# First stage of a transformer layer: modulation by row sums on three engines, two pairs of heads projected side by side

## The chip, the cores and the metric

One core of one Trainium2 chip. The metric is the device time of one execution in microseconds (us), the median over several. The engines are named as the profile names them: PE is TensorE (matmul), PEld its weight loads, DVE is VectorE, ACT is ScalarE, POOL is GpSimd, SP is SyncE, which here issues all DMAs (SPq is its queue). An engine works through its instructions in the order in which the program holds them, and waits at the first one that isn't ready.

## What is computed

One layer with stick-breaking attention and a SwiGLU FFN, float32, 2048 tokens of width 1024, 16 heads of 64, FFN width 2816. What the change touches is the first line and the modulation `h`:

```python
mod_all = jnp.einsum('bd,lde->lbe', jax.nn.silu(c), ada_w) + ada_b[:, None]
sh_m, sc_m, gt_m, sh_f, sc_f, gt_f = jnp.split(mod_all[i][:, None, :], 6, axis=-1)
h = rms_norm(x, norm_g[i, 0]) * (1 + sc_m) + sh_m
qkv = (h @ w_qkv).reshape(b, s, 3, N_HEADS, HEAD_DIM)      # then stick-breaking attention, by 128 queries
...
x = x + gt_m * rms_norm(y, norm_g[i, 1])                   # y: attention output @ w_o
h = rms_norm(x, norm_g[i, 2]) * (1 + sc_f) + sh_f
x = x + gt_f * rms_norm(swiglu_ffn(h, ...), norm_g[i, 3])
```

`sh_m` and `sc_m` are needed before the first projection: c (1024) times 2048 columns of `ada_w`, 8 MB, each element of which is used once. The other four segments come late in the attention.

## The kernel before

Tokens stand in 4 blocks of 512 (`b`), features in 8 tiles of 128 (`k` or `m`), heads in 8 pairs (`p`). Products have float32 precision by a split: each operand is a high part, written by a cast on ACT, and a low part, the rest, written by a subtraction on DVE or POOL; `mm3` (L176 to L178) makes three matmuls of it. A pair's projection `t` is 1 for k, 0 for q, 2 for v; a step (p, b) of `project` is 3 x 8 such triples, each a slice. `STEPS` orders the steps: (0, 0), (1, 0), (0, 1), (0, 2), (0, 3), (1, 1) and so on; the second one, `PARKED`, is of the second pair, and its k, q and v go to DRAM until they are needed. From (0, 1) on slices of projection are dealt out among attention units by a rate (`AHEAD`, `SLICES`, `RATE`); the first score of the attention (`score`, L604) comes after 18 slices of (0, 1). That is the same in both kernels.

The program fixes the order on PE, ACT, DVE and POOL by hand; a DMA is issued by SP in about the program's order, waiting until its tile's buffer is free. Buffers rotate under a tag (`BUFS`): "qkn" has 2, "qt" 3, "ht" 5, "kt" and "v" 7. PSUM has 8 banks: 3 of `accps` ("acc"), 3 of `zps` ("z"), 2 of `tps` ("t").

The first stage, step (0, 0):

- The modulation comes in four pieces of 256 columns (`AQ`), each of shift and scale, 2 MB in two transfers. The chunk for one k-tile is 128 rows (elements of c) by 2 x 256 columns. DVE adds the chunks up, each times its element of silu(c) (`ada_sum`, L724 and L727, 128x512), PE adds what is left along the partitions by matmuls with one column (`ada_direct` L737 with c itself, `ada_rest` L744 with ones), and `ada_cols_done` (L752 to L755) turns that into shift and gain for two feature tiles.
- Block 0 of x is squared on ACT (L167), scaled on DVE (L341), transposed on PE (`x_turn`, L372); `full_high` applies gain and shift on ACT (L782) and casts the high part (L786), `low` subtracts (L791). `weights_high` and `weights_low` (L761, L766) split the pair's three weight tiles.
- PE multiplies tile by tile of features into the three acc banks (`first_products`). SP's order: c, the first piece (2 MB), x (4 x 512 KB), the first weights (512 KB), the small constants, the other weights, the other pieces.

Step (1, 0) follows: its k goes to a z bank. Beside its slices the weights of its v are split, block 1 is squared, spread and shared (`x_square`, `x_spread`, `x_share`: a row of 512 scales, copied to all partitions by a transpose, L363 and L365), block 2 squared, and block 1's tiles are made by `first_norm` (`scale_cols` L383 on DVE and L387 on POOL, `modulate` L400 to L408). Blocks 1 and 3 come with features already along the partitions (`xc`). The evictions of k, q and v are `split` (L507 cast on ACT, L508 on DVE) and L546; `values_turn` (L552 to L557) transposes v. The k and q of (0, 0) are sent into `kt` and `qt` by four DMAs each (L524, L538), and then SP stores block 0's tiles (L482).

Of the kernel before, what the change touches and what calls it, by code (L numbers as in the profile page):

```python
# [39 lines left out]
SLICES = [0, 3 * KC] + [3 * KC + VGAP] * (NPAIR * NB - 2)  # L40


AHEAD = 6 * KC + 6
# [4 lines left out]

AQ = 256
# [25 lines left out]
SQUARE_AT = [(0, 2), (0, 7), (2, 1), (2, 7)]  # L75

NORM_AT = {
    None: [], 1: [(0, 4), (0, 6), (2, 3), (2, 5)],
    2: [(2, 2), (2, 4), (2, 6)], 3: [(2, 2), (2, 4), (2, 6)],
}  # L80
# [27 lines left out]
def hybrid_trunk_kernel(  # L108
# [5 lines left out]
    ada_first: bass.AP,  # L114
# [28 lines left out]
    shift = const.tile([P, 2, KC], F32, name="shift")  # L143
    c_act = const.tile([P, KC], F32, name="c_act")
# [61 lines left out]

    def split_early(p, t, tags):

        raw = raws.pop((p, t))
        if len(tags) == 1:  # L210
            hl = att.tile([P, 2, KC, P], F32R, name=f"w{p}_{t}", tag=tags[0], bufs=BUFS[tags[0]])
            hi, lo = hl[:, 0], hl[:, 1]
        else:
            hi, lo = [
                att.tile([P, KC, P], F32R, name=f"w{p}_{t}_{j}", tag=tag, bufs=BUFS[tag])
                for j, tag in enumerate(tags)
            ]
        nc.scalar.copy(hi, raw)
        nc.vector.tensor_tensor(lo, raw, f32(hi), op=ALU.subtract)
        weights[p, t] = hi, lo  # L220

# [167 lines left out]
    def modulate(hl, b, k):  # L389

        gain, add = g_eff[:, 0, k : k + 1], shift[:, 0, k : k + 1]
# [61 lines left out]
    def project(at):  # L453

        p, b = STEPS[at]
        begun = (p, b) == (0, 0)
# [7 lines left out]
        def product(t):  # L464
            if begun:
                return first_acc[t]
            w = weights[p, t]
            if parked and t == 1:
                acc = zps.tile([P, BT], F32, name=f"pj{p}_{b}_{t}", tag="z")
            else:  # L470
                acc = accps.tile([P, BT], F32, name=f"pj{p}_{b}_{t}", tag="acc")
            ahead = b == NB - 1 and p + 1 < NPAIR
            for k in range(KC):
                if t == 1:
                    if p == 0:
                        first_norm(b, k + (4 if b == 1 else 3))
                    if k == 0 and nb == 3:
                        cols_load(3)
                    if k == 5 and waiting:
                        waiting.pop()()  # L480
                if parked and t == 1 and k % 2 == 0:
                    nc.sync.dma_start(*stores[k // 2])  # L482
                if parked and (t, k) == (1, 6):
                    split_early(1, 2, ["whl"])
                if nb in (1, 3) and t == 1 and k < 4:
                    x_square(nb, k)
                if nb and t == 1 and 2 <= k < 6:
                    x_spread(nb, k - 2)
# [6 lines left out]
                if (t, k) in NORM_AT[nb]:  # L495
                    first_norm(nb, NORM_AT[nb].index((t, k)))
# [200 lines left out]
    chunks, piece_sums, cols_ps = {}, {}, {}  # L697

    ON_PE = {0: (0, KC - 1), 1: (KC - 1,), 2: (KC - 1,), 3: (KC - 1,)}

    def ada_chunk(q, kh):
        ks = range(KC // 2 * kh, KC // 2 * (kh + 1))
        if q == 2:
            for k in ks:
                w = att.tile([P, 2, AQ], F32, name=f"ac{q}_{k}", tag="a", bufs=BUFS["a"])
                nc.sync.dma_start(w, ada_first[q, kh][:, :, k % 4])
                chunks[q, k] = w
            return
        tag = "ht" if (q, kh) == (1, 1) else "qt"
        w = att.tile([P, 2, KC // 2, AQ], F32, name=f"ac{q}_{kh}", tag=tag, bufs=BUFS[tag])  # L710
        nc.sync.dma_start(w, ada_first[q, kh])
        for k in ks:
            chunks[q, k] = w[:, :, k % 4]
# [100 lines left out]
    for k in ada_sums(0):  # L814
        ada_sum(0, k)
# [869 lines left out]
```

## Time and profile before

| | |
|---|---|
| median of 3 runs | 2849.86 us (2848.97 to 2851.37) |
| the profiled execution's own time | 2848.15 us |
| its span on the core | 2845.8 us |
| mean granted PE clock | 0.998 |
| DMA | 521 MB, mean 183 GB/s; 262 to 414 GB/s in the stretches of 10 us of the first 60 |

How to read the rows that are shown below. A row of the timeline has start in us, length in us, engine, line, operation, output and inputs, shape, count, and in brackets the idle time before it and what ended that. A matmul's length overlaps its neighbours'; its cost is the distance to the next start. A row of the waits: who waited for whom, us in total, times, longest. A row of the groups: line, engine, operation, count, busy us and mean ns of one, then idle time before. A row of the stretches: the stretch, its length, then busy us of PE, PEld, DVE, ACT, POOL with counts, granted clock, DMA share, GB/s. A row of the DMA issues: transfer, count, KB each, us from issue to landing (median).

### The profile page before, as it was taken

The page shows a single profiled execution, that of the slowest core. Times are in us where ns is not written, and L with a number is a line of the kernel's source. Part 1 is how long each engine was busy: PE and PEld are TensorE (multiplying, and loading weights), DVE is VectorE, ACT ScalarE, POOL GpSimd, SP SyncE. Part 2 cuts the span into 40 slices and gives each one's busy share as a digit, 9 for nine tenths or more (in the row PEclk, how much of TensorE's full clock was granted, in tenths as well). Part 3 has the DMA queues.
Part 4 walks back from the last instruction along what each step waited for, and adds up shares of the span by engine and source line. Part 5 has one row for each costly group of instructions (what it writes and reads, how often), then busy time and mean ns, then how long its engine had stood idle before and what let it go on. Part 6 is the DMA issues. An engine that isn't in the chain of part 4 may idle for free.

```text
span 2845.8 us, 41691 instructions
## 1 busy us (share of the span) xinstructions
PE 2795.2 (98%) x13792; PEld 2330.7 (82%) x13792; DVE 2028.9 (71%) x2821; ACT 1634.1 (57%) x3273; POOL 1289.3 (45%) x2036
## 2 busy tenths in 40 slices
PE   8899999999999999999999999999999999999998
PEld 6688888888888888887888788888788888888887
DVE  6788888888888888888866766555775665133477
ACT  5787777787787877878645533333433333322343
POOL 2575666676576655666410122222222222544455
PEclk9999999999999999999999999999999999999999
DMA  9874556656665635546289544334353334545565
GB/s 368 283 225 164 185 161 221 211 178 226 193 211 186 216 114 178 193 134 230 95 296 317 195 141 151 119 106 158 124 177 108 111 108 163 191 142 155 179 224 185
DMA packets 240519, 521.03 MB, mean 183 GB/s; under 512 B 22448, under 2 KB 110512, under 8 KB 222640
## 3 DMA queue, kind: packets, MB, share of 16 engines
q1 hardware_dynamic: 240304, 518.38, 56.2%
q8 instruction: 109, 1.79, 0.3%
q14 instruction: 106, 0.87, 0.1%
HBM read 351.04 MB, written 118.49 MB: 165 GB/s over the span
## 4 chain that ended last, share of the span: by engine, by line
PE 86%; DVE 5%; ACT 3%; issue 2%; POOL 2%; DMA 2%; SPq 0%; DVEq 0%; POOLq 0%; ACTq 0%
PE s L176 9%; PE s L178 9%; PE s L177 9%; PE z L604 8%; PE o L683 8%; PE t L655 8%; PE pj L176 5%; PE pj L177 5%; PE pj L178 5%; PE o L177 4%; PE o L176 4%; PE o L178 4%; PE y L178 2%; PE y L176 2%; PE y L177 2%
## 5 line engine op out<-in xcount | busy, mean ns | idle before, releaser
L645 POOL TENSOR_TENSOR a<-a,w 128x512 f32<-128x512 f32 (+3 forms) x640 | 621.1, 970 | 225.2 <-DVE w L638 128.9
L638 DVE TENSOR_TENSOR_SCAN w<-z,c,begin 128x512 f32<-128x512 f32 x384 | 489.3, 1278 | 84.6 <-ACT z L623 62.2
L176 PE MATMUL s<-r,l 128*128 128x512 f32 x1232 | 482.2, 391 | 4.8 <-DVE p L1447 3.9
L178 PE MATMUL s<-r,l 128*128 128x512 f32 x1232 | 479.9, 390 | 0.0
L177 PE MATMUL s<-r,l 128*128 128x512 f32 x1232 | 479.9, 390 | 0.0
L621 ACT ACTIVATE a<-z 128x512 f32<-128x512 f32 (+3 forms) x640 | 347.4, 543 | 170.4 <-PE z L604 137.7
L683 PE MATMUL o<-aT,v 128*128 128x512 f32 (+3 forms) x1280 | 384.3, 381 | 0.1
L671 DVE TENSOR_TENSOR aT<-t,aT 128x512 fp32r<-128x512 f32 (+3 forms) x640 | 358.6, 594 | 23.7 <-ACT aT L665 23.0
L604 PE MATMUL z<-kt,qt 128*128 128x512 f32 (+3 forms) x1280 | 363.0, 365 | 0.1
L665 ACT CAST aT<-t 128x512 fp32r<-128x512 f32 (+3 forms) x640 | 314.1, 534 | 73.4 <-PE t L655 63.2
L623 ACT ACTIVATE z<-z 128x512 f32<-128x512 f32 (+3 forms) x640 | 345.0, 539 | 0.0
L1455 POOL TENSOR_TENSOR one<-p,p 128x512 f32<-128x512 f32 x44 | 71.6, 1627 | 578.1 <-issue 321.7
L176 PE MATMUL pj<-ht,w 128*128 128x512 f32 x768 | 309.1, 402 | 5.0 <-issue 1.4
L655 PE MATMUL t<-begin,a 128*128 128x128 f32 x2176 | 295.2, 273 | 14.3 <-DVE aT L671 13.0
L655 PEld LDWEIGHTS t<-begin,a 128*128 128x128 f32 x2176 | 254.7, 140 | 65.1 <-DVE aT L671 15.5
L177 PE MATMUL pj<-ht,w 128*128 128x512 f32 x768 | 303.4, 395 | 1.8 <-DVE ht L408 0.5
L178 PE MATMUL pj<-ht,w 128*128 128x512 f32 x768 | 302.8, 394 | 0.0
L176 PEld LDWEIGHTS s<-r,l 128*128 128x128 f32 x1232 | 231.7, 188 | 54.8 <-ACT l L1308 2.9
L178 PEld LDWEIGHTS s<-r,l 128*128 128x128 f32 x1232 | 231.6, 188 | 48.4
L177 PEld LDWEIGHTS s<-r,l 128*128 128x128 f32 x1232 | 231.8, 188 | 48.2 <-issue 0.5
L633 DVE TENSOR_TENSOR_SCAN w<-z,begin 128x128 f32<-128x128 f32 (+3 forms) x256 | 208.6, 817 | 76.9 <-ACT z L623 66.0
L604 PEld LDWEIGHTS z<-kt,qt 128*128 128x128 f32 x1280 | 230.3, 188 | 37.8 <-DVE w L633 0.5
(178 smaller groups left out, 4866.6 us busy)
## 6 DMA issues: line engine op xcount, KB each, us to landing
ht<-h_s SPq DMA_DIRECT2D x108, 1024.0 KB, 8.4
wi<-in_win SPq DMA_DIRECT2D x86, 512.0 KB, 4.0
qt<-qn SPq DMA_DIRECT2D x124, 256.0 KB, 4.6
ol_qt<-act_s SPq DMA_DIRECT2D x56, 512.0 KB, 3.7
act_s<-S SPq DMA_DIRECT2D x66, 256.0 KB, 3.9
br<-in_wout SPq DMA_DIRECT2D x66, 256.0 KB, 3.5
h_s<-ht SPq DMA_DIRECT2D x16, 1024.0 KB, 8.3
o_s<-os SPq DMA_DIRECT2D x128, 128.0 KB, 2.8
```

Source lines behind the costliest of these rows:

```text
L176: nc.tensor.matmul(acc, lhs[0], rhs[0], start=first, stop=False, **kw)
L177: nc.tensor.matmul(acc, lhs[0], rhs[1], start=False, stop=False, **kw)
L178: nc.tensor.matmul(acc, lhs[1], rhs[0], start=False, stop=last, **kw)
L604: nc.tensor.matmul(z[:, :n], q[:, e, part, r * P : (r + 1) * P], k[:, e, :n], start=part == 0, stop=part == 1,)
L621: nc.scalar.activation(a[:, :n], z[:, :n], AF.Sigmoid, scale=QK_SCALE)
L623: nc.scalar.activation(z[:, :n], z[:, :n], AF.Sigmoid, scale=-QK_SCALE)
L638: nc.vector.tensor_tensor_scan(rest[:, rev], left[:, rev], begin[:, :BT][:, rev], initial=carries[r], op0=ALU.mult, op1=ALU.bypass,)
L645: nc.gpsimd.tensor_tensor(a[:, :n], a[:, :n], rest[:, 1 : n + 1], op=ALU.mult)
L655: nc.tensor.transpose(pt[:, rb * P : (rb + 1) * P], weighed[i, rb][:, j * P : (j + 1) * P], ident)
L665: nc.scalar.copy(hl[:, 0, t0:], pt[:, t0:])
L671: nc.vector.tensor_tensor(hl[:, 1, t0:], pt[:, t0:], f32(hl[:, 0, t0:]), op=ALU.subtract)
L683: nc.tensor.matmul(acc[:, t0:], lhs, hl[:, part, t0:], start=sc == qb and j == 0 and part == 0, stop=sc == 0 and j == 3 and part == 1,)
```

## The change

- The modulation of the first stage is laid out by features: a row tile `ar` holds 128 features on the partitions, and shift and scale rows of 1024 (1 MB, eight of them). c comes as a row sent to all 128 partitions (`c_rows`, 512 KB). The sum along a row is one DVE instruction with an accumulator output (`row_sum`); for the shift part of tiles 1, 3, 5 and 7 POOL multiplies (`row_product`) and ACT sums (`row_total`). `row_done` makes one tile's shift and gain. PE has no part in it.
- Pairs 0 and 1 are projected side by side: for each feature tile three products for pair 0 (acc banks), then three for pair 1 (z banks). Pair 1's weights are loaded early, two of their low parts are made by POOL.
- Block 1 is loaded, squared and shared within this stage, and its first four tiles are made behind the last products' issue, ahead of the evictions of both pairs. Block 2 is squared in step (0, 1), at its q, not in (1, 0). The late parts of (1, 0) are gone: k's z bank, stores among its slices. SP sends block 0's stores partly within the stage.
- The scores' slices are the same: the 24 that are dealt to (1, 0) become 0, and `AHEAD` falls by 24.

```diff
-SLICES = [0, 3 * KC] + [3 * KC + VGAP] * (NPAIR * NB - 2)
-AHEAD = 6 * KC + 6
+SLICES = [0, 0] + [3 * KC + VGAP] * (NPAIR * NB - 2)
+AHEAD = 3 * KC + 6
...
     def project(at):
-        begun = (p, b) == (0, 0)
+        begun = at < 2
...
-            if parked and t == 1:
-                acc = zps.tile([P, BT], F32, name=f"pj{p}_{b}_{t}", tag="z")
-            else:
-                acc = accps.tile([P, BT], F32, name=f"pj{p}_{b}_{t}", tag="acc")
+            acc = accps.tile([P, BT], F32, name=f"pj{p}_{b}_{t}", tag="acc")
...
-                    if k == 5 and waiting:
-                        waiting.pop()()
+                    if k in (3, 5) and waiting:
+                        waiting.pop(0)()
...
-                if nb in (1, 3) and t == 1 and k < 4:
-                    x_square(nb, k)
-                if nb == 1 and (t, k) in SQUARE_AT:
-                    x_square(2, SQUARE_AT.index((t, k)))
+                square_at = {2: 0, 3: 1}.get(nb)
+                if t == square_at and k < 4:
+                    x_square(nb, k)
...
+    ROW_TAGS = ["whl", "qt", "qt", "qt", "ht", "qt", "qt", "qt"]
+    def row_load(m):
+        rows[m] = att.tile([P, 2, D], F32, name=f"ar{m}", tag=tag, bufs=BUFS[tag])
+        nc.sync.dma_start(rows[m], ada_rows[m])
+    def row_sum(m, seg):
+        w = rows[m][:, seg]
...
+        nc.vector.scalar_tensor_tensor(
+            w, w, 1.0, c_rows, op0=ALU.mult, op1=ALU.mult, accum_out=sums[m][:, seg : seg + 1]
+        )
+    def row_product(m):
+        w = rows[m][:, 0]
+        nc.gpsimd.tensor_tensor(w, w, c_rows, op=ALU.mult)
+    def row_total(m):
+        w = rows[m][:, 0]
+        nc.scalar.activation(w, w, AF.Identity, accum_out=sums[m][:, 0:1])
+    def row_done(m):
+        nc.vector.tensor_tensor(mod[:, :, m], sums.pop(m), b_cols[:, 0:2, m], op=ALU.add)
+        nc.vector.scalar_tensor_tensor(
+            g_eff[:, 0, m : m + 1], mod[:, 1, m : m + 1], 1.0, gc[:, 0, m : m + 1],
+            op0=ALU.add, op1=ALU.mult,
+        )
...
     nc.sync.dma_start(c_act, c)
+    c_rows = att.tile([P, D], F32, name="c_rows", tag="qkn", bufs=BUFS["qkn"])
+    nc.sync.dma_start(c_rows, c_row[0:1].to_broadcast((P, D)))
     nc.scalar.activation(c_act, c_act, AF.Silu)
-    nc.scalar.activation(spare, mhalf, AF.Sigmoid)
-    ada_chunk(0, 0)
-    ada_chunk(0, 1)
+    nc.scalar.activation(c_rows, c_rows, AF.Silu)
     x_load(0)
+    row_load(0)
     load_weights(0, 1)
     nc.sync.dma_start(b_cols, ada_b_cols)
     nc.sync.dma_start(gc, g_cols)
+    row_load(1)
     load_weights(0, 0)
     load_weights(0, 2, "qkn")
...
+    for t in (1, 0, 2):
+        load_weights(1, t, "v")
+    for m in range(2, 5):
+        row_load(m)
...
+    row_sum(0, 1)
+    row_sum(0, 0)
+    row_done(0)
+    weights_high(0, 1)
+    weights_low(0, 1, nc.vector)
+    full_high(0)
+    weights_high(0, 0)
+    low(0)
+    weights_low(0, 0, nc.vector)
+    row_sum(1, 1)
+    row_product(1)
+    weights_high(0, 2)
+    weights_low(0, 2, nc.vector)
+    row_total(1)
+    row_done(1)
+    first_products(0, 0)
+    full_high(1)
+    weights_high(1, 1)
+    weights_low(1, 1, nc.gpsimd)
+    low(1)
+    weights_high(1, 0)
+    weights_low(1, 0, nc.gpsimd)
+    turned_x[2] = x_turn(0, 2)
+    first_products(0, 1)
+    turned_x[3] = x_turn(0, 3)
+    weights_high(1, 2)
+    row_sum(2, 1)
+    weights_low(1, 2, nc.vector)
+    row_sum(2, 0)
+    row_done(2)
+    row_load(5)
+    x_load(1)
+    first_products(1, 0)
+    first_products(1, 1)
+    for m in range(2, KC):
+        full_high(m)
+        if m + 1 < KC:
+            row_sum(m + 1, 1)
+            if m % 2 == 0:
+                row_product(m + 1)
+                row_total(m + 1)
+        low(m)
+        if m + 1 < KC:
+            if m % 2 == 1:
+                row_sum(m + 1, 0)
+            row_done(m + 1)
...
+        first_products(0, m)
+        if m + 2 < KC:
             turned_x[m + 2] = x_turn(0, m + 2)
...
+        if m == KC - 1:
+            x_share(1)
+        first_products(1, m)
+    nc.sync.dma_start(*stores[0])
+    nc.sync.dma_start(*stores[1])
+    for k in range(4):
+        first_norm(1, k)
+    x_load(2)
+    nc.sync.dma_start(*stores[2])
+    nc.sync.dma_start(*stores[3])
     late = late_modulation((2, 3, 4), "wraw", 2, 0, 3, accps, "acc")
```

The evictions of both pairs follow from `project` for the first two steps, which has no slices left in them.

More of the change, by code (lines that the diff above doesn't have):

```diff
@@ L389, in modulate @@
     def modulate(hl, b, k):
-        gain, add = g_eff[:, 0, k : k + 1], shift[:, 0, k : k + 1]
+        gain, add = g_eff[:, 0, k : k + 1], mod[:, 0, k : k + 1]
         if b not in BY_FEATURES:
@@ L783, in full_high @@
             full, turned_x.pop(m), AF.Identity,
-            bias=shift[:, 0, m : m + 1], scale=g_eff[:, 0, m : m + 1],
+            bias=mod[:, 0, m : m + 1], scale=g_eff[:, 0, m : m + 1],
         )
```

202 lines of the change are left out of this document (48 added, 154 removed).

## The prediction

> **What bounds the kernel now.** I read the page, then the waits of PE (TensorE), then the first 130 us engine by engine in order of time, since the change ends there: from the first score on, both kernels issue the same work.
>
> ```profile
> span 2845.8 us, 41691 instructions
> PE 2795.2 (98%) x13792; PEld 2330.7 (82%) x13792; DVE 2028.9 (71%) x2821; ACT 1634.1 (57%) x3273; POOL 1289.3 (45%) x2036
> ```
> ```profile
> PE acol L737 <- DMA ac<-in_ada_first: 6.8, 2, 6.2
> PE t L655 <- DVE aT L671: 5.9, 4, 2.3
> ```
>
> PE is the bound: of 2845.8 us it is idle 50.6. What the first stage can give is the time before PE's first product, its slow products, and little else. The first score is the mark to which I reckon:
>
> ```profile
> 20.56 0.80 PE L176 MATMUL pj<-ht,w 128*128 128x512 f32 x1 [0.67 <-ACT ht L786]
> ...
> 27.24 0.39 PE L177 MATMUL pj<-ht,w 128*128 128x512 f32 x1
> 27.47 0.40 PE L178 MATMUL pj<-ht,w 128*128 128x512 f32 x1
> ...
> 28.70 1.05 PE L744 MATMUL acol<-ones,asum 128*128 128x1 f32 x8 [0.40 <-DVE asum L727]
> ...
> 30.04 0.63 PE L177 MATMUL pj<-ht,w 128*128 128x512 f32 x1
> 30.47 0.63 PE L178 MATMUL pj<-ht,w 128*128 128x512 f32 x1
> ```
> ```profile
> 62.05 0.39 PE L176 MATMUL pj<-ht,w 128*128 128x512 f32 x1
> ...
> 62.73 0.39 PE L176 MATMUL pj<-ht,w 128*128 128x512 f32 x1
> ...
> 72.69 0.60 PE L552 MATMUL vt<-begin,vT 128*128 128x128 f32 x4
> 73.04 0.47 PE L176 MATMUL pj<-ht,w 128*128 128x512 f32 x1
> ...
> 83.15 0.34 PE L604 MATMUL z<-kt,qt 128*128 128x128 f32 x2
> ```
>
> Three products cost 0.68 (62.05 to 62.73), four transposes 0.35 (72.69 to 73.04). In slow stretches a product takes 0.43 (30.04 to 30.47) instead of 0.23. Five tiles of the step (0,1) lie ahead of 72.69, so that step began, and both pairs of heads were done, at 72.69 - 5 x 0.68 = 69.3; the first score came 13.9 later, at 83.15.
>
> **The start.** Its transfers arrive in the order of issue:
>
> ```profile
> 10.00:20.00 10.00, 5.12 (x19) 3.66 (x18) 6.13 (x15) 7.47 (x12) 3.38 (x4) 1.00 1.03 414
> ```
> ```profile
> 9.89 1.06 ACT L167 ACTIVATE xn<-x 128x1024 f32<-128x1024 f32 x1 [5.68 <-DMA x<-in_x]
> ...
> 13.73 1.06 ACT L167 ACTIVATE xn<-x 128x1024 f32<-128x1024 f32 x1
> ...
> 15.07 1.04 ACT L761 CAST w<-wr 128x1024 fp32r<-128x1024 f32 x1 [0.19 <-DMA wr<-in_wqkv]
> ...
> 21.36 0.77 ACT L782 ACTIVATE hf<-xT,shift,g_eff 128x512 f32<-128x512 f32 x1
> 22.17 0.62 ACT L786 CAST ht<-hf 128x512 fp32r<-128x512 f32 x1
> ```
> ```profile
> 21.49 1.23 DVE L766 TENSOR_TENSOR w<-wr,w 128x1024 fp32r<-128x1024 f32 x1
> 22.82 0.69 DVE L791 TENSOR_TENSOR ht<-hf,ht 128x512 fp32r<-128x512 f32 x1
> ...
> 23.95 4.69 DVE L727 SCALAR_TENSOR_TENSOR asum<-ac,c_act,asum 128x512 f32<-128x512 f32 x6
> ```
>
> The rings are full (share 1.03, 414 GB/s). The first x tile (9.88) had 2.5 MB up to its end, the first weights (15.0) 4.5: 2.57 us a MB, so a tile lands at 3.5 + 2.57 x MB. The change puts 0.5 MB of c (one row sent to 128 partitions) where 2 MB of modulation stood: x lands from 6.1 to 9.9, row tile 0 at 12.5, the first weights at 13.8, row tile 1 at 16.3, tile 2 at 25, tile 3 at 27.5. Four squares at 1.28 (9.89 to 13.73) end at 11.3; scaling x ends at 12.9. No row shows a row sum: L727, 0.78 for 512, and 0.54 for 512 more (1.23 less 0.69) make 1.3; not under 1.23, which a product of that size takes without a sum, and not over 2.4, a rival below. Two sums, the closing pair (0.35), L782 and L786 (1.43) give the first product at 12.9 + 2.6 + 0.4 + 1.5 = 17.4, 3.2 sooner.
>
> **Between first product and the end of both pairs** the change sets POOL (GpSimd) beside DVE. That isn't free here:
>
> ```profile
> 68.39 1.44 POOL L387 TENSOR_TENSOR xc<-xc,x 128x512 f32<-128x512 f32 x1
> ```
> ```profile
> 69.17 1.20 DVE L408 TENSOR_TENSOR ht<-xc,ht 128x512 fp32r<-128x512 f32 x1 [0.50 <-ACT ht L406]
> ...
> 75.01 0.68 DVE L408 TENSOR_TENSOR ht<-xc,ht 128x512 fp32r<-128x512 f32 x1
> ```
> ```profile
> L645 POOL TENSOR_TENSOR a<-a,w 128x512 f32<-128x512 f32 x448 | 497.1, 1110 | 172.7 <-DVE w L638 128.9 <-DVE w L633 30.6 <-issue 1.9
> ...
> L204 POOL TENSOR_TENSOR w<-wr,w 128x1024 fp32r<-128x1024 f32 x21 | 50.4, 2400 | 0.0
> ```
>
> The DVE subtraction begun at 69.17 inside POOL's operation ended 0.54 after that one ended (69.83): 512 elements in 0.54, so it had stood still till then; alone it takes 0.68. Two operations that each read two tiles of SBUF run one after the other. POOL's at 1024 cost 2.2 (twice 1.11) to 2.4; I take 2.3. In order: DVE splits the first weights to 17.1; POOL's product of row tile 1 holds the port to 19.4; tile 0's low part 19.95, second weights 21.15, row sum 22.45, third weights 23.6, closing and ACT 25.4, low part 26.1, row sum of tile 2 27.4; POOL's split of pair 1's first weights 29.7; DVE's split of the third 30.85; POOL's second 33.15; row sum 34.4; POOL's product of tile 3 36.7; closing and ACT 38.5; low part of tile 2 39.2. PE, slow till about 30, has its first four parts done by 36.9 and waits till 39. Then it is the bound: two tiles cost it 4 x 2.04 + 0.7 = 8.9, and DVE and POOL together 3 x 1.3 + 1.4 + 0.7 + 2.3 = 8.3. ACT's sum over POOL's product (1.3, a square's pace) closes tile 3 at about 41, when PE needs it at 43; ACT has room there for block 1's squares and the sigmoid table, which move to it. Twelve parts are left, 24.5, four transposed tiles and the share of block 1, 1.75: end E = 39.0 + 26.2 = 65.3, against 69.3. That gain of 4.0 is all there is. The column products that go (such as the eight at 28.70), and the second slow stretch that came behind them, are inside it.
>
> **What comes behind E.** Ahead of the evictions of pair 0's three banks the new order puts the first four tiles of block 1, and these wait for the shared row, whose transposes lie only one part (2.05) before E. The banks of (0,1) are these same ones (before, a z bank kept the steps apart). On ACT (ScalarE), SP and the DMA rings:
>
> ```profile
> 50.41 0.59 ACT L507 CAST kn<-pj 128x512 fp32r<-128x512 f32 x1 [0.35 <-PE pj L178]
> ...
> 57.84 0.58 ACT L507 CAST kn<-pj 128x512 fp32r<-128x512 f32 x1
> ...
> 67.06 0.71 ACT L400 ACTIVATE ht<-xc,shift 128x512 fp32r<-128x512 f32 x1
> 67.68 0.81 ACT L405 ACTIVATE xc<-xc,shift,g_eff 128x512 f32<-128x512 f32 x1
> 68.52 0.62 ACT L406 CAST ht<-xc 128x512 fp32r<-128x512 f32 x1
> ```
> ```profile
> 51.02 2.89 SPq L524 DMA_DIRECT2D kt<-kn  x4
> 54.01 3.23 SPq L538 DMA_DIRECT2D qt<-qn  x4
> ```
> ```profile
> h_s<-ht SPq DMA_DIRECT2D x2, 1024.0 KB, 7.7
> qt<-qn SPq DMA_DIRECT2D x4, 256.0 KB, 4.5
> kt<-kn SPq DMA_DIRECT2D x4, 128.0 KB, 3.0
> ```
>
> First wait: the row is copied by E - 1.4; then DVE's scales and low parts (seven, 0.55 to 0.74) and POOL's four scales (1.1) alternate at the port, and the eviction of k comes last: 4.3 + 4.4 + 0.7, so PE gets a bank at E + 8.0 (E + 5.5 if nothing blocked). Second wait: pair 1's k (the eviction at 57.84 before, 7 us behind pair 0's) takes the buffer from which pair 0's k is still being sent. Those four transfers are issued from E + 8.0 over 2.9 and land 3.0 behind the start of the last: E + 13.2. On SP they stand behind block 0's stores and block 2's loads, sent by E + 3, and behind block 1's first two stores of 1 MB, which wait for the low parts of tiles 1 and 3 (E + 7.3); at 2.57 a MB these are through by then, at the 7.7 of the row above 2 us later. Pair 1's q waits likewise for four more, issued over 3.2, landing 4.5 behind (median; 2.57 by bytes alone): E + 16.8. Queued behind it on ACT: pair 1's v and block 1's tiles 4 to 7, which (0,1) needs at its fifth tile. Two pairs at 0.62 + 0.84 + 0.52, two evictions and the last low part bring the eighth tile's products to E + 23.1. Eight tiles more, 5.46, two more, 1.37: first score at E + 30. Before, this stretch took 13.9.
>
> PE stands still for 8 us in it, so part of its products may go at 0.43: the light stretch from 27.7 to 30 sufficed for that. I count up to 1.5 for it, and it lies in the range. [...]
>
> **Sum.** First score 65.3 + 30.0 = 95.3 against 83.15: +12.1. Behind it the same slots follow. PE lost 5.9 there to DVE (the second wait row), beside transfers that in the new order are mostly done earlier; between 0 and 3 of it may go, I take 1. So +11: the profiled execution's own 2848.15 becomes 2859.2; it stood 1.7 below the median of 2849.86, so the median would be 2861.
>
> **Rivals.**
> No blocking at the port: POOL and DVE overlap. For it: only a few rows show blocking. The stage then ends at 61.3 (PE alone, slow till 30) and the score comes at E + 27.4: 88.7, +5.5; 2855.4 with the 1.7 added.
> Faster: the stage runs at PE's pace and the evictions come in time. From 17.4, 144 products (32.6) and seven groups of transposes (2.5) at full pace end at 52.5; with some slow products 58. If both waits behind E together stay at 3 us, the score is at 58 + 13.9 + 3 = 75: -8, 2842 with the 1.7 added. It decides where the waits behind E stay under 83.15 - 13.9 - E, 4.0 at my E. Against it: the order of ACT and DVE alone makes 5.5.
> Row sums at half pace: nothing in the trace sums along a row on DVE while it multiplies two tiles. At 2.4 each, the chain to 39.2 grows by 5 x 1.1, and two tiles cost the port 11.6 against PE's 8.9, 2.7 for each of two and a half pairs: about +12 more, 2873. [...]
> The change doesn't do what it says: c's row to 128 partitions is slow. Everything behind it in the rings shifts, the start's 3.2 is lost and some more: 2865.
>
> **How the numbers follow.** Forecast 0.55, no blocking 0.18, half pace 0.12, faster 0.10, slow row 0.05. The forecast's own range is 2855 to 2867: E by 2 either way (POOL at 2.2 or 2.4, PE slow till 30 or 33), the transfers by 2, the clock by 1.5. To hold 8 in 10 it reaches down past the case without blocking, 2853, and up to 2868. 0.2%, 5.7 us, is about what a measurement can tell from no change: above 2855.6 lie most of the forecast, some of the case without blocking, and the two slow ones, 0.76; below 2844.2 the faster case, 0.10; between, 0.14.
>
> **What would show it.** Right: first product near 17.4; DVE operations of over 1.3 beside POOL's between 17 and 37; PE idle some 8 us between the last product of pair 1 and (0,1), released by DVE's eviction of k; ACT's eviction of pair 1's k and q waiting for DMA kt and qt; first score near 95. Wrong: a first score before 83, PE idle under 3 us behind E, or row sums near 2.4.

## The result, and the profile after

The changed kernel takes 2868.69 us (median of 4, 2867.20 to 2870.23) against 2850.61 for the kernel before (median of 4): a ratio of 1.0064, 95% interval 1.0046 to 1.0081. It is slower by 18.1 us. The direction was forecast, the size was not: 11 us, and the measured time lies 0.7 above the range. The profiled execution took 2870.23, its span is 22.5 longer than before's. That is more than the 18.1 of the medians, because the changed kernel's profiled execution is the longest of its four and before's (2848.15) is shorter than all of its runs; the marks below are read from these two. The page of the profile after, and PE's waits in its first 200 us:

```profile
span 2868.3 us, 41549 instructions
PE 2793.8 (97%) x13720; PEld 2326.2 (81%) x13720; DVE 2038.7 (71%) x2816; ACT 1639.8 (57%) x3282; POOL 1306.3 (46%) x2042
```
```profile
PE xT L351 <- DVE xn L320: 13.7, 4, 11.4
PE pj L171 <- DVE kn L479: 8.1, 1, 8.1
PE pj L171 <- ACT ht L738: 6.0, 3, 2.9
PE t L626 <- DVE aT L642: 5.8, 4, 2.3
PE vt L523 <- DVE kn L479: 3.5, 1, 3.5
PE pj L171 <- ACT ht L379: 3.3, 1, 3.3
```

PE is busy as long as before (2793.8 against 2795.2); all of the loss is idle time. Three of these rows lie behind the stage: 8.1, 3.5 and 3.3. The wait for aT, of which the forecast gave back 1, is what it was (5.8 against 5.9). In order of time on PE:

```profile
19.36 0.80 PE L171 MATMUL pj<-ht,w 128*128 128x512 f32 x1 [2.87 <-ACT ht L738]
...
41.50 0.51 PE L171 MATMUL pj<-ht,w 128*128 128x512 f32 x1 [2.31 <-ACT ht L738]
...
78.74 0.79 PE L171 MATMUL pj<-ht,w 128*128 128x512 f32 x1 [8.09 <-DVE kn L479]
...
86.49 1.12 PE L523 MATMUL vt<-begin,vT 128*128 128x128 f32 x4 [3.54 <-DVE kn L479]
...
92.20 0.80 PE L171 MATMUL pj<-ht,w 128*128 128x512 f32 x1 [3.32 <-ACT ht L379]
...
104.66 0.33 PE L575 MATMUL z<-kt,qt 128*128 128x128 f32 x2
```

First product 19.36 (forecast 17.4), tile 2 at 41.50 (39.0), E, the stage's end, at 78.74 - 8.09 = 70.65 (65.3), first score at 104.66 (95.3; before 83.15). So 5.4 of the error lies before E and 4.0 behind it. As a second mark I take PE's longest wait in the attention's first diagonal blocks, the same wait in both:

```profile
126.69 0.33 PE L655 MATMUL t<-begin,a 128*128 128x128 f32 x1 [2.28 <-DVE aT L671]
```
```profile
148.29 0.48 PE L626 MATMUL t<-begin,a 128*128 128x128 f32 x1 [2.26 <-DVE aT L642]
```

It is 21.6 later, the first score 21.5: nothing comes back and little is added between the two.

### The profile page after: what moved, and what is told of

It reads as the page before. It is cut to its first block, busy times and chain, and to the rows that moved or that the text cites. A ratio compares the mean times of both kernels' runs of the same rounds, so it can differ in the third digit from the quotient of the medians.

```text
span 2868.3 us, 41549 instructions
## 1 busy us (share of the span) xinstructions
PE 2793.8 (97%) x13720; PEld 2326.2 (81%) x13720; DVE 2038.7 (71%) x2816; ACT 1639.8 (57%) x3282; POOL 1306.3 (46%) x2042
## 5 line engine op out<-in xcount | busy, mean ns | idle before, releaser
L626 PEld LDWEIGHTS t<-begin,a 128*128 128x128 f32 x2176 | 255.9, 141 | 62.1 <-DVE aT L642 13.2
```

What stands on the lines that cost most here:

```text
L626: nc.tensor.transpose(pt[:, rb * P : (rb + 1) * P], weighed[i, rb][:, j * P : (j + 1) * P], ident)
```

## The experiments

E is the end of the last product of the stage, "later" the second mark; both and the first score are from each kernel's profile, one execution each. The changed kernel, e1, e2, e3 and e15 have the same work up to E, and their E lies between 68.87 and 71.89: that two kernels differ by 1 or 2 us there says little by itself.

| run | ratio to before, 95% interval | E | first score | later |
|---|---|---|---|---|
| before | 1 | - | 83.15 | 126.69 |
| changed | 1.0064, 1.0046 to 1.0081 | 70.65 | 104.66 | 148.29 |
| e1_order | 1.0033, 1.0021 to 1.0046 | 70.62 | 94.62 | 138.23 |
| e2_buffers | 1.0060, 1.0046 to 1.0073 | 70.84 | 94.10 | 143.75 |
| e3_both | 1.0031, 1.0020 to 1.0043 | 71.89 | 92.42 | 139.81 |
| e15_scale_dve | 1.0058, 1.0046 to 1.0071 | 68.87 | 100.89 | 144.51 |
| e11_tail_only | 1.0019, 1.0010 to 1.0028 | 71.94 | 89.86 | 136.26 |
| e4_no_pool | 1.0057, 1.0044 to 1.0069 | 65.93 | 100.20 | 143.81 |
| e5_c_pe | 1.0069, 1.0056 to 1.0081 | 70.50 | 104.73 | 148.31 |
| e8_rows_only | 1.0009, 1.0000 to 1.0018 | - | 86.89 | 130.79 |
| e14_rows_no_pool | 0.9997, 0.9988 to 1.0005 | - | 84.19 | 127.72 |
| e6_early_share | 1.0038, 1.0025 to 1.0050 | 67.00 | 94.34 | 137.88 |
| e7_all | 1.0019, 1.0010 to 1.0028 | 62.76 | 90.19 | 135.18 |
| e9_tail_and_stage | 0.9987, 0.9978 to 0.9996 | 61.62 | 79.43 | 124.89 |
| e12_c_transfer | 0.9990, 0.9981 to 0.9998 | 63.84 | 83.04 | 128.59 |
| e10_warm | 0.9983, 0.9974 to 0.9991 | 60.48 | 78.51 | 124.92 |
| e13_v_later | 1.0017, 1.0008 to 1.0026 | 60.33 | 74.58 | 133.32 |
| e16_v_before_loads | 0.9988, 0.9979 to 0.9997 | 60.29 | 74.62 | 124.89 |

### Which part of the change loses: e8 and e14

```diff
 # the kernel before, its ada_chunk/ada_sum/ada_rest replaced by the change's row_load .. row_done
-    for q in range(4): ...            # two feature tiles at a time
+    for m in range(2, KC): ...        # as in the change, first_products(m) for pair 0 alone
 # e14 besides: row_sum(m, 0) for row_product and row_total; c's row as in e5
```

> One part of the change by itself: the kernel before with its modulation as row sums on three engines, tile by tile (DVE, POOL and ACT as in the change), but with one pair of heads in the first stage and the second pair's first step behind it, in the order of before. Theory (the loss lies in the stretch behind the two pairs, the row sums cost about what they bring): about 4 us of DVE and POOL a tile bound the stage of eight tiles, which ends near 50 as before; first score 82 to 87, 2847 to 2853, a ratio of 0.999 to 1.0015. Rival (the row sums, with the blocked port and the slow row of c, make most of the loss): first score over 92, ratio 1.003 or more.

> Row sums by themselves once more (one pair of heads in the first stage, order of before), now without POOL in the stage (all row sums on DVE) and with c's row spread by TensorE. Theory (DVE's two row sums, low part and closing, 3.8 us a tile, bound a stage with 2.05 us of products a tile; two pairs side by side are what fills TensorE beside them): the stage still ends near 48, first score 82 to 86, ratio 0.999 to 1.001, slower than the reordered kernel with two pairs by 0.001 or more. Rival (side by side brings nothing, DVE instead of POOL and the shorter start do it all): first score near 78, ratio 0.997 to 0.9985.

The row sums alone cost 0.0009 (2.6 us): on the theory's side, and far from the 18. Their stage did not end as early as expected, though: ACT begins the eviction of pair 0's k at 54.97, against 50.41 in the kernel before. Without POOL and with the shorter start it begins at 52.28, and the time is even with before (0.9997). That leaves most of the loss to the second pair in the first stage and to what it does to the order behind it, which e11 tests.

### The stretch behind the stage: e1, e2, e3, e15, e11

```diff
 # e1: order
-    for k in range(4):
-        first_norm(1, k)
     x_load(2)
...
     def project(at):
+        if at == 1:
+            for k in range(4): first_norm(1, k)
```
```diff
 # e2: buffers of pair 1's k and q; e3 has both edits
-    hl = att.tile(..., tag="qkn", ...)
+    place = "wraw" if parked else "qkn"
+    hl = att.tile(..., tag=place, ...)
```

> Only the order changes: block 1's first four tiles are issued behind pair 0's evictions and ahead of pair 1's, instead of ahead of both. Theory (the evictions queued behind block 1's tiles, then the buffers of pair 1's k and q, make the loss): PE's 8.1 us behind pair 1's last product shrink to 3 to 5, since it still waits for block 1's first tile; pair 0's k and q leave 7 us sooner, so pair 1's k and q get their buffers sooner too, and the first score comes 5 to 7 us sooner, near 98.5: 2863. Rival (the transfers or the clock alone decide when the first score comes): 2867 to 2870, no difference from the changed kernel.

Half of the loss is gone (1.0064 to 1.0033), more than expected. The 8.1 became 2.5 for block 1's first tile and 1.8 for its low part.

> Order as in the changed kernel; pair 1's k and q go to two buffers that are free at that time (tag wraw) instead of those from which pair 0's k and q are still being sent. Theory: the first wait of 8.1 us stays, the second (ACT 8.4 and 4.7 us for the transfers of kt and qt, with block 1's tiles 4 to 7 queued behind) goes; first score 6 to 9 us sooner: 2860 to 2863. Rival (the transfers only fill time in which ACT and DVE would be late anyway): under 2 us, 2867 or more.

The first score came 10.6 sooner than in the changed kernel, the time only 1 (0.0004, within the intervals): on the time the rival was right. The buffers that I took are those in which block 2 is squared, and these squares on ACT now waited 3.5 us for the store of pair 1's k. A first score alone is not yet a gain.

> Both edits. Theory: the two waits are in one chain, so the gains add up less than fully: first score 10 to 13 us sooner, near 93: 2856 to 2859, still slower than before by 6 or more, since the stage itself ended 1.3 later than before's and block 1's tiles come late. Rival (one of the two hides the other): no better than the better of the two alone.

No better than e1 alone (1.0031, intervals overlap): its first score is 2.2 sooner than e1's, but ACT's squares of block 2 wait for the stores of pair 1's k and q here too (1.65 and 0.18), and the later mark is no better. The rival was right, by a wait that the edit itself brought.

```diff
 # e15: scale_cols and modulate, block 1
-        if k % 2 == 0:
+        if k % 2 == 0 or b == 1:
```

> The changed kernel with one edit: block 1's odd tiles are scaled on DVE (with the factor in the same operation) instead of on POOL. The prediction held that the order of ACT and DVE alone makes 5.5 us of the first wait behind the stage and the blocked port the other 2.5. Theory: PE's wait falls from 8.1 to 5 to 6; the second wait starts sooner by as much, first score near 102: ratio 1.005 to 1.006. Rival (the wait is the order's alone, DVE needs the time that POOL needed): wait 7.5 or more, ratio 1.0062 or more.

```profile
73.11 0.50 PE L171 MATMUL pj<-ht,w 128*128 128x512 f32 x1 [4.24 <-ACT vT L517]
```
```profile
74.08 0.69 DVE L479 TENSOR_TENSOR kn<-pj,kn 128x512 fp32r<-128x512 f32 x1
```

The eviction of k ended at 74.77, 5.9 behind E (68.87), where the forecast had 5.5 without blocking, a figure for which it shows no sum. It is not quite the same case: DVE makes three scales more than in the changed kernel ahead of this eviction, and works from 67.45 without a pause. So the run agrees with the forecast's split of the 8.0 into order and POOL (at least 2.2 of the 8.1 go without POOL), but does not measure it. PE started sooner still, 4.24 behind E, because its product now took v's bank, which ACT copies without DVE. The time fell by 0.0006 only, within the intervals: ACT's waits for the transfers of kt and qt, 7.6 and 4.4, stood behind it. E is 1.8 sooner here with the stage untouched, so of the 3.8 by which the first score is sooner 2.0 lie behind E.

For e11 the whole stretch is reordered, the stage's own work left as it is:

```diff
-        if m in (5, 6):  x_square(1, ...)            # and x_spread at m == 6
+        if m in (4, 5):  x_square(1, ...)            # and x_spread at m == 5
-        if m == KC - 1:  x_share(1)                  # before pair 1's products
+        if m == KC - 2:  x_share(1)                  # before pair 0's products
...
     def projections():
-            yield from project(at)
+            if at != 1: yield from project(at)
...   # in (0, 1), product(1)
+                    if at == 2 and k == 4:
+                        for _ in project(1): pass    # pair 1's evictions, behind block 1's tiles
...
+    place = "v" if parked else "qkn"                 # buffers of pair 1's k and q
-    pool, ptag = (zps, "z") if early else (accps, "acc")
+    pool, ptag = (tps, "t") if early else (accps, "acc")
 # and e15's edit
```

> The changed kernel with its stage as it is (POOL's products and splits, c's row by transfer), and only the stretch behind it reordered: shared row, tiles of block 1 during pair 1, evictions of pair 1 inside (0,1) to buffers of their own, odd tiles scaled on DVE. Theory (that stretch makes 14 to 18 of the 21.5 by which the first score was late): stage ends at 70 to 71 as in the changed kernel, first score 14 to 16 later, at 84 to 87: a ratio of 1.0005 to 1.0015. Rival (POOL and DVE are too busy in the stage to make block 1's tiles meanwhile): first score at 90 to 94, ratio 1.003.

```profile
71.55 0.39 PE L173 MATMUL pj<-ht,w 128*128 128x512 f32 x1
71.98 0.50 PE L171 MATMUL pj<-ht,w 128*128 128x512 f32 x1
...
78.96 1.12 PE L527 MATMUL vt<-begin,vT 128*128 128x128 f32 x4 [2.62 <-ACT vT L521]
```
```profile
71.33 0.60 ACT L521 COPY vT<-pj 128x512 f32<-128x512 f32 x1
```
```profile
72.96 0.68 DVE L483 TENSOR_TENSOR kn<-pj,kn 128x512 fp32r<-128x512 f32 x1
```

The step (0, 1) follows the stage without any wait. Pair 0's banks are complete one part before E, and ACT has copied v's bank by 71.93, just before E (71.94). DVE ends its part of k's eviction at 73.64 only, so the first product must have taken v's bank here, as in e15, and not k's, as in the changed kernel. The first score comes 17.9 behind E (expected 14 to 16; one wait of 2.6 and slow products behind it, 0.43 apart from 80.30 on, are left), and the ratio falls from 1.0064 to 1.0019, 13 of the 18 us. That is the order, the buffers and the other bank together; no run takes the bank by itself.

### The stage itself: e4 and e5

```diff
 # e4
-    row_product(1)
...
-    row_total(1)
+    row_sum(1, 0)
...                                                   # likewise tiles 3, 5, 7
-    weights_low(1, 1, nc.gpsimd)                     # and (1, 0)
+    weights_low(1, 1, nc.vector)
 # e5
-    nc.sync.dma_start(c_rows, c_row[0:1].to_broadcast((P, D)))
+    nc.sync.dma_start(c_one[0:1], c_row)
+    for half in range(2):                            # products with ones, K = 1, into two z banks
+        nc.tensor.matmul(ps, ones[0:1], c_one[0:1, sl], start=True, stop=True)
+        nc.scalar.activation(c_rows[:, sl], ps, AF.Silu)
```

> No large operation of POOL in the first stage: the products of row tiles 1, 3, 5, 7 and their sums on ACT become row sums on DVE, and the low parts of pair 1's first two weights are DVE's too. Theory (DVE stands still while POOL reads two tiles): the chain to tile 2 loses about 9 us of POOL and of stopped DVE time and gains 5 of DVE, so tile 2's products begin 4 to 5 us sooner, near 37, and the stage ends 3 to 5 us sooner; the stretch behind it stays: 2864 to 2866. Rival (no exclusion, POOL's work was free): DVE gets 7.4 us more work, and the time is the same or up to 4 us longer.

What POOL did to DVE in the changed kernel (POOL's queue, then DVE's), and the same closing operations in e4:

```profile
27.92 6.36 POOL L718 TENSOR_TENSOR w<-wr,w 128x1024 fp32r<-128x1024 f32 x2 [6.78 <-ACT w L714]
34.24 5.67 POOL L688 TENSOR_TENSOR ar<-ar,c_rows 128x1024 f32<-128x1024 f32 x2
```
```profile
32.01 3.35 DVE L682 SCALAR_TENSOR_TENSOR ar<-ar,c_rows 128x1024 f32<-128x1024 f32 x1
35.29 0.08 DVE L682 DVE_READ_ACCUMULATOR ar<-ar,c_rows 128x1 f32 x1
35.40 2.20 DVE L695 TENSOR_TENSOR mod<-as,b_cols 128x2 f32<-128x2 f32 x1
37.64 2.28 DVE L696 SCALAR_TENSOR_TENSOR g_eff<-mod,gc 128x1 f32<-128x1 f32 x1
```
```profile
34.82 0.16 DVE L695 TENSOR_TENSOR mod<-as,b_cols 128x2 f32<-128x2 f32 x1
35.02 0.16 DVE L696 SCALAR_TENSOR_TENSOR g_eff<-mod,gc 128x1 f32<-128x1 f32 x1
```

An operation on two elements per partition takes 0.16 by itself and 2.20 beside POOL, the next one, on a single element, 2.28 instead of 0.16; that one ends where POOL's second product ends (39.92 against 39.91). Each waits for an operation of POOL's. Without POOL the gain of tile 2 is ready 4.7 sooner, and E comes 4.7 sooner. The time falls by little (1.0064 to 1.0057), below what was expected, though the first score was 4.5 sooner; the intervals overlap widely and leave room for more. With the stretch behind mended, the same edit is worth more: e12 against e11 (with one cast of ACT moved besides) is 0.9990 against 1.0019, with E 8.1 sooner.

> One edit of the changed kernel: c's row is loaded as one row of 4 KB and spread to 128 partitions by two products of TensorE with ones (into two z banks, from which ACT makes the silu), instead of by a transfer that writes it to 128 partitions. Theory (that transfer keeps the rings busy for over 3 us while they move 127 to 201 GB/s, and all that follows shifts): x lands 2 to 3 us sooner, first product near 16.5 instead of 19.4, tile 2's products 2 to 3 sooner, and the time falls by 2 to 3, to a ratio near 1.0056. Rival (what decides is the port, whatever the start): the first product comes sooner, but tile 2 does not, and the time stays within 1 us.

The changed kernel's stretches from 3 to 5 us, and then e5's:

```profile
3.00:4.00 1.00, 0.00 (x0) 1.00 1.04 127
4.00:5.00 1.00, 0.00 (x0) 1.00 0.95 201
```
```profile
3.00:4.00 1.00, 1.00 (x2) 1.00 0.76 266
4.00:5.00 1.00, 1.00 (x2) 1.00 1.02 410
```

The last two columns are DMA share and GB/s. The transfer of one row to 128 partitions keeps the rings busy (1.04 and 0.95) at a third to a half of the 410 GB/s that e5's second stretch shows. How slow it is differs between executions: in e15, which has the same transfer, it is 164 and 279 GB/s, and ACT's silu of c starts at 5.67 there, at 6.77 in the changed kernel. Without it x's first square starts 1.1 sooner (6.97 instead of 8.07), and yet the first product is not sooner, 19.60: POOL's product now starts sooner too, ahead of DVE's closing operation, which it stops. e5's POOL, then DVE:

```profile
15.66 2.34 POOL L688 TENSOR_TENSOR ar<-ar,c_rows 128x1024 f32<-128x1024 f32 x1 [3.17 <-DMA ar<-in_ada_rows]
```
```profile
15.80 2.21 DVE L696 SCALAR_TENSOR_TENSOR g_eff<-mod,gc 128x1 f32<-128x1 f32 x1
```

The wait for POOL gave the start back: the rival was right on the time (no gain), though by another way than it said, for tile 2's products did come 1.0 sooner (40.45), and E is the same (70.50).

### Putting it together: e6, e7, e9, e12, e10, e13, e16

> The run without POOL in the first stage, with the stretch behind it reordered: block 1's squares, spreads and shared row come one feature tile sooner, so that its first four tiles are made while PE still works on pair 1; pair 1's evictions are issued behind block 1's eighth tile, inside the step (0,1), and the transposes of v go to the other PSUM banks (tag t), since the z banks are released late. Theory (only the order of the evictions and of block 1's tiles makes the 34 us from the stage's end to the first score, before it was 13.9): the stage ends at 65 to 67, the wait behind it is under 2 us, the first score comes 14 to 17 later, at 80 to 83: 2844 to 2849, a ratio of 0.999 to 1.000. Rival (block 1's tiles take DVE time from the stage, which DVE bounds here): the stage ends 4 later, first score near 88, ratio 1.002.

e6 is e4 with a first form of e11's order (shared row before pair 1's products of tile 6, buffers left in qkn, odd tiles on POOL). It missed: E at 67.00 was as expected, but 3.0 of wait stand behind it (POOL's scales again stop DVE: in e7, which has the same scales, two of DVE's take 3.48 beside them, and in e15 three take 2.08 without) and 6.7 for v, behind ACT's wait of 4.4 for the transfers of qt; the first score is later than even the rival had it.

> The same reordered kernel without POOL in the first stage, with c's row spread by TensorE, and ACT's cast of pair 1's first weights moved ahead of tile 1. Theory: 3 us from the start and up to 2 from DVE's wait at tile 1 come on top, first score at 75 to 79: 2840 to 2845, a ratio of 0.997 to 0.999, faster than before. Rival (DVE bounds the stage from tile 2 on, and the transfers of the row tiles, which arrive in their order, set when): not over 1 us better than the run before it.

e7 adds e5's edit and moves ACT's cast of the weights (1, 1) ahead of `full_high(1)`. E came 4.2 sooner and the first score as well; the waits behind E are those of e6, so it missed in the same way: 1.0019 instead of 0.999 at most.

> The last reordered kernel (no POOL in the first stage, c's row spread by TensorE) with three edits where its trace still shows waits: block 1's shared row is made another half tile sooner, block 1's odd tiles are scaled on DVE with the factor in the same operation instead of on POOL (which stopped DVE for 3.5 us there), and pair 1's k and q go to two buffers of the tag v instead of those still being sent (ACT had waited 1.3 and 4.6 us for them, and PE 6.9 behind that). Theory: the stage ends near 61, the wait behind it falls from 3.0 to 1.4, the one for v goes; first score at 75 to 78, 5 to 8 sooner than the kernel before: 2840 to 2844, a ratio of 0.9975 to 0.999. Rival (a wait that comes next takes their place, k's transfers or DVE): first score over 82, ratio 1.000 or more.

e9 has all of e11's reordering, e4, e5 and the moved cast. It is faster than before: 0.9987. The chain of the forecast is gone: E at 61.62, the first product of (0, 1) at 61.66. The wait for v was to go as well, but stays at 2.6, and the first score comes at 79.43 instead of 75 to 78.

```profile
61.23 0.39 PE L173 MATMUL pj<-ht,w 128*128 128x512 f32 x1
61.66 0.50 PE L171 MATMUL pj<-ht,w 128*128 128x512 f32 x1
...
68.64 1.12 PE L527 MATMUL vt<-begin,vT 128*128 128x128 f32 x4 [2.62 <-ACT vT L521]
...
79.43 0.33 PE L580 MATMUL z<-kt,qt 128*128 128x128 f32 x2
```

> The reordered kernel without POOL in the stage and with the three new edits, but c's row brought by the transfer to 128 partitions as in the changed kernel. Theory (that transfer costs 2 us at the start, and with POOL gone nothing eats them): first product and first score 1.7 to 3 later than with TensorE's products, ratio 0.0006 to 0.001 higher. Rival (DVE's row sums bound the stage from tile 2 on and absorb the start): within 0.5 us.

With c's transfer put back the first product comes 2.2 later (19.80 against 17.57), E 2.2 and the later mark 3.7. Other kernels bear out the start: without POOL the first product comes at 19.54 to 19.80 with the transfer (e4, e6, e12) and at 17.57 to 17.84 with TensorE's products (e7, e9, e14). The medians of eleven runs do not show it (0.9990 against 0.9987, either interval 0.0009 to each side): inconclusive on the time, plain in the traces.

```diff
 # e10
+    for _ in range(3):                               # and 2 more before first_products(0, 1)
+        nc.tensor.matmul(first_acc[1, 2], ones, begin[:, :BT], start=True, stop=True)
     first_products(0, 0)
```

> The same, with five products of zeros and ones put on TensorE where it stands still before the first product (three) and before tile 1 (two), into a bank that is cleared later; they compute nothing that is used. Theory (the slow products till about 29 are the clock's, and idle time makes the clock slow): the granted clock is full from the first product on, products take 0.23 instead of 0.43 from 17.8 to 29; since tile 1 and the weights arrive in that time anyway, the stage ends 1 to 2 sooner, ratio 0.0004 to 0.0007 lower. Rival (the arrival of data decides): no difference over 0.5 us.

The products followed: from the second one on they are 0.23 to 0.30 apart where e9's are 0.43 apart. e9's first, then e10's:

```profile
19.31 0.63 PE L171 MATMUL pj<-ht,w 128*128 128x512 f32 x1
19.74 0.63 PE L172 MATMUL pj<-ht,w 128*128 128x512 f32 x1
```
```profile
18.46 0.46 PE L172 MATMUL pj<-ht,w 128*128 128x512 f32 x1
18.76 0.40 PE L173 MATMUL pj<-ht,w 128*128 128x512 f32 x1
19.00 0.40 PE L171 MATMUL pj<-ht,w 128*128 128x512 f32 x1
```

That this is the clock is argued: the granted clock reads 1.00 from 17 to 29 us in both runs, and only later slow stretches, such as the changed kernel's from 42 to 44 (0.51), show it. The idle products can hold up what follows them: in e13 and e16, which keep them, the first product comes right behind them at 18.30 and 18.78, against 17.57 in e9. E and the first score come 1.1 and 0.9 sooner; the later mark is the same (124.92 against 124.89), and the ratio 0.9983 against 0.9987 is not told apart. It is the lowest ratio here, 0.0017 (4.8 us) below the kernel before.

```diff
 # e13, then e16 in its place: the second values_turn
-                    if k in (3, 5) and waiting:
+                    if k == 3 and waiting:
...
+                if (t, k) == (0, 1) and waiting: waiting.pop(0)()     # e13, behind x_load(3)
+                if (t, k) == (0, 0) and waiting: waiting.pop(0)()     # e16, ahead of x_load(3)
```

> The kernel with TensorE's idle products, with one more edit behind the stage: the transposes of pair 1's v stand in front of the second tile of q instead of the sixth tile of k, where TensorE had waited 2.6 us for ACT's copy and then ran slowly. Theory (what is left of the stretch behind the stage above 13.9 is this wait and the slow clock it brings): first score 3 to 4.5 sooner, at 74 to 75.5, ratio 0.9965 to 0.9975. Rival (a later wait, the transfers of k or block 2's squares on ACT, takes over): first score within 1 us of the run before, ratio 0.998.

The first score came 3.9 sooner, as expected, and the kernel lost 0.0034. v's tile was now allocated behind block 3's loads and got the buffer from which k was being stored; ACT stood there, with block 2's squares queued behind it, and PE for block 2's tiles:

```profile
81.84 0.59 ACT L533 CAST v<-vt 128x512 fp32r<-128x512 f32 x1 [8.39 <-DMA k_park<-kn]
```
```profile
85.43 0.48 PE L351 MATMUL xT<-begin,x 128*128 128x128 f32 x1 [10.52 <-DVE x L328]
```

> The run before with its mistake mended: there, the transposes of pair 1's v stood behind the loads of block 3 in the order of issue, so that v's tile got the buffer from which pair 1's k was still being stored, and ACT, with block 2's squares queued behind, stood 8.4 us for it (TensorE 10.5 behind that). Now they stand in front of those loads, ahead of q's first tile. Theory: the first score stays at 74.5 to 75.5, and block 2's tiles come in time: a ratio of 0.9965 to 0.998, faster than the kernel before by 6 to 10. Rival (a further wait takes over again, so that this stretch cannot be shortened below that of the kernel with TensorE's idle products): 0.998 to 0.999.

The wait for k's store is gone, the first score stays at 74.62, and the time is e10's within the intervals (0.9988): the rival was right. Of the 3.9, 3.2 went into waits of block 2's transposes for DVE, whose input ACT squares.

```profile
77.09 0.47 PE L351 MATMUL xT<-begin,x 128*128 128x128 f32 x1 [2.14 <-DVE x L328]
```

The traces show why the squares are no sooner. They stand on ACT behind the eviction of the k of (0, 1), and that waits until 72 in both kernels for a buffer from which kt is being sent. e10's eviction, then e16's:

```profile
72.19 0.59 ACT L482 CAST kn<-pj 128x512 fp32r<-128x512 f32 x1 [3.27 <-DMA kt<-kn]
```
```profile
71.98 0.59 ACT L484 CAST kn<-pj 128x512 fp32r<-128x512 f32 x1 [4.72 <-DMA kt<-kn]
```

With first scores at 79.43, 78.51 and 74.62, e9, e10 and e16 reach the later mark at 124.89, 124.92 and 124.89. They are level by 101.5 already, at a score for which e9 and e10 wait for a transfer of qt, 0.83 and 0.97. e10's row, then e16's:

```profile
101.53 0.41 PE L580 MATMUL z<-kt,qt 128*128 128x128 f32 x2 [0.97 <-DMA qt<-qn]
```
```profile
101.48 0.41 PE L582 MATMUL z<-kt,qt 128*128 128x128 f32 x2
```

So the transfers of kt and qt take the place of what was mended. In e16 the DMA share is 0.97 to 1.02 in each stretch of 20 us from 20 to 100. That earlier transfers would bring the later mark forward was not tried.

## Why the prediction was right or wrong

The direction and the chain of causes were right; terms of the sum were too small. The first score came 9.4 later than forecast: 0.5 of it are what is left of a late start, 2.0 DVE's waits for POOL, 2.9 the stretch from tile 2 to E, 4.0 the stretch behind E.

**The start: wrong by 2.0.** The step that failed is the reckoning of transfers by bytes, 2.57 us a MB. c's row took the rings at 127 and 201 GB/s, landed just before 6.77, where ACT's silu of it starts (5.67 to 7.19 in the other runs that have this transfer), while 4.8 follows from its bytes, and all behind it shifted. This is the rival "slow row", held at 0.05; its mechanism came, its price did not, since the start matters little while DVE's waits for POOL decide (e5).

**Row sums: right.** By itself each took 1.22, and 0.08 for its accumulator: 1.3 as forecast. The rival at half pace falls: no run shows the 2.4 that it put in. Of the twelve sums on DVE eleven took 1.21 to 1.22, and the one that took longer, 3.35, stood beside POOL.

```profile
15.02 1.22 DVE L682 SCALAR_TENSOR_TENSOR ar<-ar,c_rows 128x1024 f32<-128x1024 f32 x1
16.16 0.08 DVE L682 DVE_READ_ACCUMULATOR ar<-ar,c_rows 128x1 f32 x1
```

**POOL beside DVE: the waiting right, the term too small.** POOL and DVE ran one after the other (e4 shows the cause: E comes 4.7 sooner without POOL), so the rival without blocking falls. The traces show the waiting alone; "port" is my name for it, and that the two share one is not shown. But POOL's two splits took 3.2 each, not 2.3, and the closing pair 4.5. The forecast has 0.35 for the pair and one product of POOL's (2.3) ahead of it: I had put the pair down as work, and not as two operations that each wait for one of POOL's. POOL had two products to do there, those of tiles 3 and 5 (5.67 together), and each of the two closing operations waited for one. POOL's first split of pair 1 began at 27.92, where the forecast has 27.4, so most of the late start was absorbed by then; tile 2's product came at 41.50 instead of 39.0, and the 2.0 that came in between are this term. Operations of other sizes waited too: the low part of tile 0 takes 2.35, begun at 19.34 inside POOL's first product, that of tile 1 takes 0.69 without.

**Tile 2 to E: 2.9 too short.** The forecast let PE be slow till 30. It waited again at tile 2 (2.31), and the next products, from 42.23 to 45.38, are 0.43 apart (the first 0.59) instead of 0.23, 1.5 in all, at a granted clock of 0.51 from 42 to 44; another 0.5 is the wait for tile 2's low part, the rest is spread over the other parts. The step that failed is "slow till about 30".

**Behind E: the chain right in every link, 4.0 too short.** The bank came at E + 8.1 (forecast 8.0), by the order forecast; e15, which gives POOL's scales to DVE, has the eviction done at E + 5.9, near the forecast's split. ACT's evictions of pair 1 waited for kt and qt as said, but at E + 14.5 and E + 19.8 instead of 13.2 and 16.8:

```profile
78.53 4.12 SPq L495 DMA_DIRECT2D kt<-kn  x4
82.75 3.21 SPq L509 DMA_DIRECT2D qt<-qn  x4
```
```profile
85.12 0.59 ACT L478 CAST kn<-pj 128x512 fp32r<-128x512 f32 x1 [8.44 <-DMA kt<-kn]
...
90.45 0.59 ACT L478 CAST qn<-pj 128x512 fp32r<-128x512 f32 x1 [4.74 <-DMA qt<-qn]
```

The four issues of kt took 4.1, not 2.9, and q landed 4.5 behind the end of its last issue (85.96), where the forecast's numbers leave 2.7. The forecast had taken the middle between the 4.5 of its own row, counted from the start of an issue, and 2.57 by bytes. That makes 3.0 of the 4.0. The rest fits the clock: after the idle 8.1 PE's products stay 0.43 apart through two more waits, till 96.3 (granted clock 0.50 from 88 to 96), so that the eighth tile's products begin at 97.15, 0.95 behind the end of its low part (96.20). The prediction counted up to 1.5 for slow products, in its range alone. The slow ones are the first nine behind the 8.1 (granted clock 0.50 from 79 to 83) and those of the fourth to the sixth tile of the first eight; the second eight tiles run 0.23 apart.

**Behind the first score: 1 was taken as a gain and did not come** (5.8 of wait for aT against 5.9).

**The rival "faster"** named the right condition, waits under 4 behind the stage. e11 has no wait at E and 2.6 later; with POOL gone too, e12 and e9 are faster than before. What the changed kernel lost is therefore two things, each taken away by itself on top of the other: the order and buffers behind the stage, the bank included, 0.0045 (e11), and POOL beside DVE in the stage, 0.0029 (e12 against e11, with the one moved cast). Together they exceed the loss; what is left is a gain of 0.001. Whether that gain is the second pair's is not settled: e9 and e14 differ by 0.001, with overlapping intervals.

## What to carry to other kernels

When work is put in front of evictions, follow every buffer that they free, not only the first: here one wait for a bank, one for a buffer being sent and one for ACT's queue stood behind each other, and mending one showed the next. Count the smallest operations of an engine that another one stops, for here they waited like the large ones (128x2 took 2.20 instead of 0.16, 128x512 2.35 instead of 0.69); and choose a mark behind all that the change moves, since a first score 8.5 sooner was worth 3.4 (e16).

## What the hardware showed that I had not expected

- One row of 4 KB sent to 128 partitions keeps the rings busy (share 1.04 and 0.95) at 127 to 201 GB/s in the changed kernel's trace, where the loads behind it reach 415 to 422.
- A DVE operation on 128x1 or 128x2 takes 0.16, and 2.2 to 2.3 when POOL works on two tiles of 1024 (the changed kernel, e5). POOL's own take 2.3 to 2.7 singly and 2.8 to 3.2 where several follow each other with DVE in between.
- Five idle products on zeros, put where TensorE stands still, brought the products behind them from 0.43 to 0.23 apart (e10), though the granted clock reads 1.00 there with and without them.
